# A SwiGLU down projection with seven products for eight in seven of its eleven chunk pairs, summed inside the PSUM banks

## The chip, the cores and the metric

One core of one Trainium2 chip runs the whole kernel in one launch. The metric is the device time of one execution in microseconds; the kernel before takes 1071.21 us (median of three runs, 1068.43 to 1071.74). The engines are TensorE (PE, with its weight loads as PEld), VectorE (DVE), ScalarE (ACT), GpSimd (POOL) and SyncE (SP), which here only issues DMAs.

## What is computed

A decoder trunk of two layers on 512 tokens of width 1024, in float32. Layer 0 mixes with two kinds of attention, layer 1 with pooling; each layer then has a SwiGLU block. The change is in the last product of that block, which runs twice:

```python
def swiglu(h, w_gate, w_up, w_down):
    return (jax.nn.silu(h @ w_gate) * (h @ w_up)) @ w_down   # 512x1024 -> 512x2816 -> 512x1024
...
    h = h + rmsnorm(swiglu(u, ffn_w_gate[layer], ffn_w_up[layer], ffn_w_down[layer]), g[3])
```

The down product multiplies the 512 x 2816 activations by a 2816 x 1024 weight. The 2816 are 22 chunks of 128, taken in 11 pairs.

## The kernel before, in words

**Three matmuls for one product.** PE multiplies in a reduced format, so every float32 operand is split in two: a high half (ACT copies it, rounding) and a low half (the source minus the high half, a subtraction on DVE or POOL). `conv` (L242 to L245) does it for weights, `split` (L219 to L221) for activations. A product is then high x high, high x low and low x high: three matmuls.

**Gate and up.** `Ffn.run` (L933) goes through the 11 pairs of hidden chunks, gate and up in turn, with seven products for eight (Strassen, in Winograd's form): DVE forms sums of weight blocks (`comb`, L913) and of results (L962 to L964, L972), `up_done` (L981 to L987) writes the activations `act`, two tiles of 128 x 512 for a pair: hidden on the partitions, tokens along the row.

**Down.** `down` (L776) has eight PSUM banks, one for each of four token tiles and two halves of the output (tags `psT`, `psO` for half 0, `psA`, `psS` for half 1). It runs through all 22 chunks for half 0, then the first 14 chunks for half 1, and keeps the last eight chunks' weights of half 1 in `wrh`, `wrl`; the returned `tail(t)` finishes one token tile after the other, so that the norm behind can begin. For each chunk, token tile and half there are three matmuls of 128 x 512 (L782 to L784): 22 x 8 x 3 = 528. Activations are split by `split` on ACT and DVE; the low halves of the weights go to POOL and DVE by the pattern `ggv` (two on POOL, one on DVE).

**What sets the order.** The kernel is written with tile pools; a scheduler orders the instructions of each engine when the program is built, and each engine then runs its own list in that order. A buffer of a pool comes free with its last reader. The pools that matter: `wr` (11 raw weight tiles, filled by SP's DMAs), `wq` (14 split weights), `g` (31 tiles), `xe` (4), `jk` (2) and, in attention, `sc` (2).

## Time and profile before

| | us |
|---|---|
| median of three runs | 1071.21 |
| the profiled execution | 1071.16 |
| its span, first to last instruction | 1069.4 |
| PE busy / DVE / ACT / POOL | 1023.3 / 755.3 / 563.0 / 314.5 |
| the two down products, start of the first matmul | 553.08 and 942.64 |

The page's slices show PE at 97% to 100% nearly everywhere, a mean granted clock of 0.987 of full speed, and DVE at 90% or more in the gate and up stages. A matmul's record is longer than its share of the engine, since matmuls overlap: the distance from one start to the next is what one costs in a full stream. The same holds for DVE and ACT records. A view of waits names the instruction that was late, and for whom.

### The profile page before, as it was taken

How to read it: one execution, taken by the hardware profiler on the slowest of the kernel's cores; microseconds unless marked ns; L12 is line 12 of the kernel's file. 1: busy time of each engine (PE TensorE's matmuls, PEld its weight loads, DVE VectorE, ACT ScalarE, POOL GpSimd, SP SyncE). 2: the span in 40 equal slices, each digit the busy share in tenths (PEclk: the TensorE clock that was granted, in tenths of full speed). 3: DMA queues.
4: the chain of work that ended last, by engine and by line, in shares of the span. 5: the costliest groups of instructions: out<-in, count | busy, mean ns of one | idle time of the engine just before them, and what ended most of it. 6: DMA issues, size and time to landing. Idle time of an engine off the chain costs nothing.

```text
span 1069.4 us, 19004 instructions
## 1 busy us (share of the span) xinstructions
PE 1023.3 (96%) x6892; PEld 940.4 (88%) x6892; DVE 755.3 (71%) x1527; ACT 563.0 (53%) x1194; POOL 314.5 (29%) x282
## 2 busy tenths in 40 slices
PE   6999999997999999999999999988999999999997
PEld 5788978896888999999988888988999999978886
DVE  5338898758749999899973153998898898881204
ACT  6437688769656454454564352764444354472401
POOL 5713666767751000000026371420000000053510
PEclk9999999999999999999999999998999999999999
DMA  8841201323531434433343374003342333433302
GB/s 244 195 96 40 60 21 32 95 73 102 169 89 31 119 109 116 123 102 107 119 153 114 106 218 110 21 11 92 97 138 83 112 114 90 139 117 121 108 1 78
DMA packets 156493, 108.58 MB, mean 102 GB/s; under 512 B 14836, under 2 KB 137584, under 8 KB 156400
## 3 DMA queue, kind: packets, MB, share of 16 engines
q1 hardware_dynamic: 155600, 106.23, 34.6%
q8 instruction: 54, 0.88, 0.4%
q10 hardware_dynamic: 800, 1.15, 0.3%
q14 instruction: 39, 0.32, 0.1%
HBM read 101.88 MB, written 2.10 MB: 97 GB/s over the span
## 4 chain that ended last, share of the span: by engine, by line
PE 77%; DVE 8%; ACT 5%; issue 3%; DMA 3%; POOL 2%; SPq 1%; DVEq 0%; POOLq 0%; ACTq 0%
PE psS L944 8%; PE psS L945 8%; PE psS L946 7%; PE psA L944 5%; PE psA L945 5%; PE psA L946 5%; PE psT L784 2%; PE psO L784 2%; PE psT L782 2%; PE psT L783 2%; PE psO L783 2%; PE psO L782 2%; PE psA L782 2%; PE psA L784 2%; PE psA L783 2%
## 5 line engine op out<-in xcount | busy, mean ns | idle before, releaser
L244 ACT ACTIVATE wh<-wr 128x512 fp32r<-128x512 f32 x376 | 226.3, 626 | 256.8 <-DVE wr L913 82.4
L245 POOL TENSOR_TENSOR wl<-wr,wh 128x512 fp32r<-128x512 f32 x101 | 145.4, 1449 | 556.5 <-ACT wh L244 329.8
L245 DVE TENSOR_TENSOR wl<-wr,wh 128x512 fp32r<-128x512 f32 x275 | 189.5, 706 | 92.1 <-ACT wh L244 89.4
L944 PE MATMUL psS<-th,wh 128*128 128x256 f32 x528 | 149.8, 285 | 1.3 <-DVE comb L964 1.3
L945 PE MATMUL psS<-tl,wh 128*128 128x256 f32 x528 | 150.0, 285 | 0.0
L946 PE MATMUL psS<-th,wl 128*128 128x256 f32 x528 | 149.9, 284 | 0.0
L944 PEld LDWEIGHTS psS<-th,wh 128*128 128x128 f32 x528 | 101.6, 193 | 1.6 <-DVE comb L964 0.9
L945 PEld LDWEIGHTS psS<-tl,wh 128*128 128x128 f32 x528 | 101.8, 193 | 0.0
L946 PEld LDWEIGHTS psS<-th,wl 128*128 128x128 f32 x528 | 101.7, 193 | 0.0
L913 DVE TENSOR_TENSOR wr<-wr,wr 128x512 f32<-128x512 f32 x132 | 86.7, 682 | 1.3 <-DMA wr<-in_ffn_w_up_dram 0.5
L946 PE MATMUL psA<-uh,wl 128*128 128x256 f32 x272 | 77.5, 286 | 3.1 <-DVE wl L245 3.0
L944 PE MATMUL psA<-uh,wh 128*128 128x256 f32 x272 | 77.5, 286 | 2.1 <-DVE comb L962 1.7
L945 PE MATMUL psA<-ul,wh 128*128 128x256 f32 x272 | 77.3, 284 | 0.0
L270 POOL TENSOR_SCALAR E<-E,ri 128x128 f32<-128x128 f32 (+3 forms) x48 | 56.0, 1167 | 38.8 <-DVE ri L590 12.9
L584 ACT ACTIVATE E<-E,mn 128x128 f32<-128x128 f32 (+1 forms) x96 | 53.4, 557 | 15.7 <-DVE mn L582 15.0
L946 PEld LDWEIGHTS psA<-uh,wl 128*128 128x128 f32 x272 | 52.6, 194 | 3.5 <-DVE wl L245 3.5
L944 PEld LDWEIGHTS psA<-uh,wh 128*128 128x128 f32 x272 | 52.5, 193 | 2.7 <-DVE comb L962 2.1
L332 PE MATMUL psA<-uh,wh 128*128 128x512 f32 (+1 forms) x136 | 51.4, 378 | 1.7 <-DVE nq L464 1.5
L945 PEld LDWEIGHTS psA<-ul,wh 128*128 128x128 f32 x272 | 52.6, 193 | 0.0
L221 DVE TENSOR_TENSOR pl<-psT,ph 128x512 fp32r<-128x512 f32 (+1 forms) x72 | 42.3, 593 | 12.5 <-ACT ph L220 8.7
L334 PE MATMUL psA<-uh,wl 128*128 128x512 f32 (+1 forms) x136 | 50.9, 374 | 0.0
L333 PE MATMUL psA<-ul,wh 128*128 128x512 f32 (+1 forms) x136 | 50.7, 373 | 0.0
(354 smaller groups left out, 3009.8 us busy)
## 6 DMA issues: line engine op xcount, KB each, us to landing
wr<-in_ffn_w_gate_dram SPq DMA_DIRECT2D x98, 256.0 KB
wr<-in_ffn_w_up_dram SPq DMA_DIRECT2D x98, 256.0 KB
wr<-in_ffn_w_down_dram SPq DMA_DIRECT2D x88, 256.0 KB
wr<-in_attn_w_in_dram SPq DMA_DIRECT2D x40, 256.0 KB
wr<-in_attn_w_out_dram SPq DMA_DIRECT2D x16, 256.0 KB
x<-in_x_dram SPq DMA_DIRECT2D x4, 512.0 KB
gbc<-in_norm_g_dram SPq DMA_DIRECT2D x8, 256.0 KB
h<-in_x_dram SPq DMA_DIRECT2D x4, 512.0 KB
```

Source lines behind the costliest of these rows:

```text
L244: nc.scalar.activation(hi, src, AF.Copy)
L245: next_engine(key).tensor_tensor(lo, src, r32(hi), op=ALU.subtract)
L270: (nc.vector if k == "v" else nc.gpsimd).tensor_scalar(e, e, s1, None, op0=ALU.mult)
L332: nc.tensor.matmul(psum, wh, ah, start=first, stop=False)
L584: nc.scalar.activation(e, e, AF.Exp, bias=mn[:, n_:n_ + 1], scale=-1.0, accum_out=sm[:, n_:n_ + 1])
L782: nc.tensor.matmul(o, acts[c][0][:, tok], wh[k], start=first, stop=False)
L783: nc.tensor.matmul(o, acts[c][0][:, tok], wl[k], start=False, stop=False)
L784: nc.tensor.matmul(o, acts[c][1][:, tok], wh[k], start=False, stop=last)
L913: next_engine("sadd").tensor_tensor(o, x0, x1, op=op)
L944: nc.tensor.matmul(o, wh, bh, start=start and k == 0, stop=False, skip_group_check=True)
L945: nc.tensor.matmul(o, wh, bl, start=False, stop=False, skip_group_check=True)
L946: nc.tensor.matmul(o, wl, bh, start=False, stop=k == 3, skip_group_check=True)
```

## The change

Seven of the eleven pairs (`nst=7`) of the down product are done with seven products for eight. For a pair, with e and o its even and odd activation tile (tokens 0 to 255 and 256 to 511) and b11, b12 (even chunk), b21, b22 (odd chunk) the blocks of the weight, a product is 256 tokens by 512 outputs: two token tiles, six matmuls of 128 x 512.

- `act_sums` forms three sums of activation blocks for each of the seven pairs, on DVE, as soon as the pair's activations are there (128 x 256 each), so in the gate and up stage.
- `down` is a method of its own. A first pass over the seven pairs does four products of each into four pairs of banks (C11 in `psO`, C22 in `psT`, C21 in `psA`, C12 in `psS`), added up over the seven pairs. Then the sums between the products are made once, in the banks: for each of two bank numbers two copies on ACT and four additions on DVE. A second pass does the other three products of each pair. The four remaining pairs are plain: half 0 first, half 1 from kept weights in `tail(t)`, as before.
- For each pair DVE makes three weight sums (L1049, `sub`) in the first pass, and one weight sum and one activation sum in the second; six operands are split in the first pass and five in the second, all low halves on DVE (pattern `v`); none of down's go to POOL any more.
- The block b22 is loaded in both passes: five loads of 256 KB for such a pair in place of four.
- Pools: `g` has 33 tiles, `jk` 3, and `sc` is now taken from `jk`. The bank tags of the pooling mixer change with the banks that come free.

```diff
--- before.py
+++ after.py
@@ -32,13 +32,14 @@
     norm='vggvgvvg',
     wlo0='g',
     wlo1='ggv',
-    ng=31,
+    ng=33,
     no=8,
     xe=4,
     pt=4,
     w=14,
     wr=11,
-    jk=2,
+    jk=3,
+    nst=7,
     psb=(2, 2, 2, 2),
     early=('kc', 'vc'),
     hpe=50,
@@ -60,7 +61,7 @@
     plo='vvv',
     lead=0,
     tr2='W0 T0 T1 E0 T2 E1 B0 T3 E2 E3 W1 B1 M0 M1 F0 F1 B2 M2 B3 R0 M3 A0 F2 F3 R1 Z A1',
-    ptags=(('psO', 'psA'), ('psO', 'psS')),
+    ptags=(('psO', 'psS'), ('psO', 'psA')),
 )
 OFF = {}
 _o = 0
@@ -148,7 +149,7 @@
         return T(shape, "pt", CFG["pt"], dt, label)
 
     def SC():
-        return T([P, S], "sc", 2, F32, "sc")
+        return JK("sc")
 
     def SM(shape, label="sm"):
         return T(shape, "sm", 16, F32, label)
@@ -840,6 +841,7 @@
             self.uns = []
             self.acts = {}
             self.ws = {}
+            self.S = {}
             self.g = bcast(norm_g[layer, 2], "g2", where)
 
         def weights(self, p):
@@ -992,6 +994,8 @@
                     gate_done(ms[i])
                 else:
                     up_done(todo[i][0], ms[i - 1], ms[i])
+                    if pairs.index(todo[i][0]) < CFG["nst"]:
+                        self.act_sums(todo[i][0])
 
             gens = [self.pair_weights(w_, p) for p, w_ in todo]
             ws = [next(gens[0])]
@@ -1009,25 +1013,115 @@
                 middle(ms[i])
             finish_(len(todo) - 1)
 
-            wres = T_([P, 8, S], "uh", 1, F32R, "wrh"), T_([P, 8, S], "ul", 1, F32R, "wrl")
-            pos = []
-
-            def take(shape):
-                pos.append(0)
-                k = len(pos) - 1
-                return tuple(w_[:, k:k + 1, :] for w_ in wres)
-
-            def get(c):
-                if c >= 20:
-                    t_ = XE([P, 2, S], F32R, label="asp")
-                    hi, lo = t_[:, 0, :], t_[:, 1, :]
+            return self.down(pairs)
+
+        def act_sums(self, p):
+
+            e, o = self.acts[2 * p], self.acts[2 * p + 1]
+            a11, a21, a22 = e[:, 0:256], e[:, 256:], o[:, 256:]
+            t_ = G([P, S], label="as")
+            s1, s3 = t_[:, 0:256], t_[:, 256:]
+            nc.vector.tensor_add(s1, a21, a22)
+            nc.vector.tensor_sub(s3, a11, a21)
+            nc.vector.tensor_sub(a21, s1, a11)
+            self.S[p] = t_
+
+        def down(self, pairs):
+
+
+
+
+            w = w_down[self.layer]
+            n = CFG["nst"]
+            C11, C22, C21, C12 = ([BANK(tag) for _ in range(2)] for tag in ("psO", "psT", "psA", "psS"))
+            out_ = {(t, m): ((C11, C12) if t < 2 else (C21, C22))[m][t % 2] for t in range(NT) for m in range(2)}
+
+            def raw(p, k, m):
+                c = 2 * p + k
+                return load_raw(w[c * P:(c + 1) * P, m * S:(m + 1) * S].rearrange("(k p) f -> p k f", p=P), [P, 1, S])[0][:, 0, :]
+
+            def put(src, pair=None):
+                hi, lo = pair or WQ2([P, S])
+                conv(hi, lo, src, "slo")
+                return hi, lo
+
+            def sub(o, x0, x1):
+                nc.vector.tensor_tensor(o, x0, x1, op=ALU.subtract)
+
+            def prod(o, a, b, first=False, last=False):
+                (ah, al), (bh, bl) = a, b
+                nc.tensor.matmul(o, ah, bh, start=first, stop=False, skip_group_check=True)
+                nc.tensor.matmul(o, ah, bl, start=False, stop=False, skip_group_check=True)
+                nc.tensor.matmul(o, al, bh, start=False, stop=last, skip_group_check=True)
+
+            def tile_of(a, j):
+                return tuple(x_[:, j * P:(j + 1) * P] for x_ in a)
+
+            t2s = {}
+            for i, p in enumerate(pairs[:n]):
+                b11, b12, b22 = raw(p, 0, 0), raw(p, 0, 1), raw(p, 1, 1)
+                t1, t2s[p] = JK("t1"), G([P, S], label="t2")
+                e_, s_ = (XE([P, 2, S], F32R, label=l_) for l_ in ("ae", "as"))
+                conv(e_[:, 0, :], e_[:, 1, :], self.acts[2 * p], "slo")
+                w11 = put(b11)
+                sub(t1, b12, b11)
+                sub(t2s[p], b22, t1)
+                w2 = put(t2s[p])
+                sub(b12, b22, b12)
+                conv(s_[:, 0, :], s_[:, 1, :], self.S[p], "slo")
+                w3 = put(b12)
+                w1 = put(t1)
+                ends = i == 0, i == n - 1
+                for o, a, c0, b in ((C11, e_, 0, w11), (C22, e_, 256, w2), (C21, s_, 256, w3), (C12, s_, 0, w1)):
+                    for j in range(2):
+                        prod(o[j], (a[:, 0, c0 + j * P:c0 + (j + 1) * P], a[:, 1, c0 + j * P:c0 + (j + 1) * P]), b, *ends)
+            for j in range(2):
+                x_, y_ = JK("u2"), JK("u3")
+                nc.scalar.activation(x_, C11[j], AF.Copy)
+                nc.vector.tensor_add(x_, C22[j], x_)
+                nc.vector.tensor_add(y_, C21[j], x_)
+                nc.scalar.activation(C21[j], y_, AF.Copy)
+                nc.vector.tensor_add(C22[j], C12[j], y_)
+                nc.vector.tensor_add(C12[j], C12[j], x_)
+            for i, p in enumerate(pairs[:n]):
+                b21, b22 = raw(p, 1, 0), raw(p, 1, 1)
+                e, o = self.acts[2 * p], self.acts[2 * p + 1]
+                o_ = XE([P, 2, S], F32R, label="ao")
+                s_ = G([P, 2, 256], F32R, label="s4")
+                conv(o_[:, 0, :], o_[:, 1, :], o, "slo")
+                w21 = put(b21)
+                sub(t2s[p], b21, t2s[p])
+                w4 = put(t2s[p])
+                sub(e[:, 256:], o[:, 0:256], e[:, 256:])
+                conv(s_[:, 0, :], s_[:, 1, :], e[:, 256:], "slo")
+                w22 = put(b22)
+                for c_, a, b in ((C11, (o_[:, 0, 0:256], o_[:, 1, 0:256]), w21), (C21, (o_[:, 0, 256:], o_[:, 1, 256:]), w4),
+                                 (C12, (s_[:, 0, :], s_[:, 1, :]), w22)):
+                    for j in range(2):
+                        prod(c_[j], tile_of(a, j), b)
+            chunks = [2 * p + k for p in pairs[n:] for k in range(2)]
+            nr = len(chunks)
+            acts = []
+            for i, c in enumerate(chunks):
+                if i < 6:
+                    pair = tuple((C if i < 2 else G)([P, S], F32R, label=l_) for l_ in ("ah", "al"))
                 else:
-                    f = G if c < 10 or c >= 16 else O if c < 14 else C
-                    hi, lo = (f([P, S], F32R, label=n_) for n_ in ("ah", "al"))
-                split(hi, lo, self.acts[c])
-                return hi, lo
-
-            return down(get, NF, w_down[self.layer], lambda i: take)
+                    x_ = XE([P, 2, S], F32R, label="asp")
+                    pair = x_[:, 0, :], x_[:, 1, :]
+                conv(pair[0], pair[1], self.acts[c], "slo")
+                acts.append(pair)
+                b = put(raw(c // 2, c % 2, 0))
+                for t in range(NT):
+                    prod(out_[t, 0], tile_of(pair, t), b, False, i == nr - 1)
+            wres = [T([P, 8, S], tag, 1, F32R, "wres") for tag in ("uh", "ul")]
+            held = [put(raw(c // 2, c % 2, 1), tuple(x_[:, i, :] for x_ in wres)) for i, c in enumerate(chunks)]
+
+            def tail(t):
+                for i in range(nr):
+                    prod(out_[t, 1], tile_of(acts[i], t), held[i], False, i == nr - 1)
+                return [out_[t, 0], out_[t, 1]]
+
+            return tail
 
     T_ = T
     phase["wlo"] = CFG["wlo1"]
```

The scheduler's lists of DVE and PE change as follows, here in the first of the two blocks (the second reads alike). In these rows `wh`/`wl` are the high and low half of a weight, `ae`, `as`, `ao`, `s4` split activations of the passes, `al` the low half of a plain chunk's activation, `t1`, `t2` weight sums, `u2`, `u3` the sums in the banks, `comb` gate and up's results. Lines of the kernel after: L246 low half, L974 the last addition of gate and up, L988 and L989 the last activations, L1049 `sub`, L1081 to L1085 the sums in the banks, L1053 to L1055 high x high, high x low, low x high.

DVE where gate and up end and down begins, before:

```order
L972 TENSOR_TENSOR comb_22_7093<-psS_109_7092,comb_22_7093 128x512
L986 TENSOR_TENSOR act_21_7210<-comb_21_6988,comb_22_7093 128x256
L987 TENSOR_TENSOR act_22_7211<-comb_21_6988,comb_22_7093 128x512
L221 TENSOR_TENSOR al_1_7234<-act_1_4123,ah_1_7233 128x512
L221 TENSOR_TENSOR asp_1_7673<-act_21_7210,asp_1_7673 128x512
```

The same place in the kernel after:

```order
L974 TENSOR_TENSOR comb_22_7121<-psS_109_7120,comb_22_7121 128x512
L988 TENSOR_TENSOR act_21_7238<-comb_21_7016,comb_22_7121 128x256
L989 TENSOR_TENSOR act_22_7239<-comb_21_7016,comb_22_7121 128x512
L1049 TENSOR_TENSOR t2_1_7258<-wr_167_7255,t1_1_7257 128x512
L1049 TENSOR_TENSOR t2_2_7315<-wr_170_7312,t1_2_7314 128x512
L1049 TENSOR_TENSOR t2_3_7372<-wr_173_7369,t1_3_7371 128x512
L246 TENSOR_TENSOR ae_2_7316<-act_1_4123,ae_2_7316 128x512
L246 TENSOR_TENSOR as_9_7317<-as_2_5004,as_9_7317 128x512
L246 TENSOR_TENSOR wl_200_7270<-t2_1_7258,wh_200_7269 128x512
```

Where `al_1`, which the first chunk needs, stood right behind the last activations, three weight sums and two low halves now stand ahead of `wl_200`, which the second product of the first pair needs.

DVE between the two passes, in the kernel after; the list is continuous, and these are its 89th to 100th instruction from the L974 above:

```order
L246 TENSOR_TENSOR s4_7_7923<-act_13_6244,s4_7_7923 128x256
L246 TENSOR_TENSOR al_3_8005<-act_17_6794,ah_3_8004 128x512
L246 TENSOR_TENSOR al_4_8027<-act_18_6795,ah_4_8026 128x512
L1082 TENSOR_TENSOR u3_1_7651<-psA_52_7247,u2_1_7650 128x512
L1049 TENSOR_TENSOR t2_7_7600<-wr_198_7918,t2_7_7600 128x512
L246 TENSOR_TENSOR al_5_8049<-act_19_7067,ah_5_8048 128x512
L1081 TENSOR_TENSOR u2_2_7658<-psT_97_7246,u2_2_7658 128x512
L246 TENSOR_TENSOR al_6_8071<-act_20_7068,ah_6_8070 128x512
L246 TENSOR_TENSOR wl_234_7764<-t2_3_7372,wh_234_7763 128x512
L246 TENSOR_TENSOR wl_235_7771<-wr_191_7752,wh_235_7770 128x512
L246 TENSOR_TENSOR al_2_7983<-act_16_6522,ah_2_7982 128x512
L246 TENSOR_TENSOR wl_236_7801<-wr_192_7792,wh_236_7800 128x512
```

Five low halves of plain chunks (`al`), which no matmul needs before the second pass is over, stand ahead of `wl_236`, which the second pass's fourth pair needs.

PE at the place that needs it, in the kernel after; the fourth row is the 198th of the 486 matmuls of down:

```order
L1053 MATMUL psA_52_7247<-wh_234_7763,ao_3_7754 128x512
L1054 MATMUL psA_52_7247<-wl_234_7764,ao_3_7754 128x512
L1055 MATMUL psA_52_7247<-wh_234_7763,ao_3_7754 128x512
L1054 MATMUL psO_37_7243<-wl_236_7801,ao_4_7796 128x512
L1055 MATMUL psO_37_7243<-wh_236_7800,ao_4_7796 128x512
L1054 MATMUL psO_38_7244<-wl_236_7801,ao_4_7796 128x512
L1053 MATMUL psS_110_7249<-wh_229_7686,s4_1_7671 128x512
```

From this row on 289 matmuls of down follow, itself included.

## Rows read from the trace of the kernel before

**Rows 1.** The page's busy times (us, share of the span, instructions).

```profile
PE 1023.3 (96%) x6892; PEld 940.4 (88%) x6892; DVE 755.3 (71%) x1527; ACT 563.0 (53%) x1194; POOL 314.5 (29%) x282
```

**Rows 2.** Busy time by stretch: PE, PEld, DVE, ACT, POOL, granted clock, DMA share, GB/s.

```profile
500.00:530.00 30.00, 30.00 (x252) 30.00 (x251) 28.17 (x52) 15.16 (x28) 0.00 (x0) 1.00 0.39 114
560.00:590.00 30.00, 30.00 (x134) 24.82 (x134) 11.52 (x22) 14.22 (x27) 19.49 (x8) 1.00 0.36 114
960.00:990.00 30.00, 30.00 (x134) 24.82 (x134) 5.23 (x7) 6.99 (x12) 10.78 (x8) 1.00 0.40 124
```

**Rows 3.** PE's waits from 330 to 1064 us: total, times, longest.

```profile
PE psA L946 <- DVE wl L245: 3.0, 1, 3.0
PE psT L782 <- ACT ah L220: 2.3, 2, 1.2
...
PE psT L784 <- DVE al L221: 0.4, 2, 0.2
```

**Rows 4.** Timeline of PE, the second down: start, length, idle before.

```profile
941.19 0.28 PE L946 MATMUL psS<-uh,wl 128*128 128x256 f32 x1
942.64 0.50 PE L782 MATMUL psT<-wh,ah 128*128 128x512 f32 x1 [1.17 <-ACT ah L220]
...
944.96 0.50 PE L784 MATMUL psT<-wh,al 128*128 128x512 f32 x1 [0.21 <-DVE al L221]
...
1062.05 0.39 PE L784 MATMUL psS<-wrh,asp 128*128 128x512 f32 x1
...
1062.73 0.39 PE L784 MATMUL psS<-wrh,asp 128*128 128x512 f32 x1
```

**Rows 5.** Timeline of DVE, instructions in close succession.

```profile
500.31 0.41 DVE L964 TENSOR_TENSOR comb<-psS,comb 128x256 f32<-128x256 f32 x1
500.64 0.68 DVE L245 TENSOR_TENSOR wl<-wr,wh 128x512 fp32r<-128x512 f32 x1
...
558.88 7.91 DVE L221 TENSOR_TENSOR al<-act,ah 128x512 fp32r<-128x512 f32 x13
```

**Rows 6.** Timeline of DVE at the end of the first gate and up.

```profile
542.65 0.69 DVE L245 TENSOR_TENSOR wl<-wr,wh 128x512 fp32r<-128x512 f32 x1 [0.99 <-ACT wh L244]
...
545.77 0.69 DVE L245 TENSOR_TENSOR wl<-wr,wh 128x512 fp32r<-128x512 f32 x1 [1.56 <-ACT wh L244]
...
551.94 0.69 DVE L972 TENSOR_TENSOR comb<-psS,comb 128x512 f32<-128x512 f32 x1 [1.50 <-PE psS L946]
552.66 1.47 DVE L986 TENSOR_TENSOR act<-comb,comb 128x256 f32<-128x256 f32 x1
554.06 0.68 DVE L987 TENSOR_TENSOR act<-comb,comb 128x512 f32<-128x512 f32 x1
```

**Rows 7.** DVE's groups by shape, 350 to 545 us: busy us, mean ns, idle.

```profile
L245 DVE TENSOR_TENSOR wl<-wr,wh 128x512 fp32r<-128x512 f32 x112 | 74.3, 683 | 3.6 <-ACT wh L244 3.5
...
L972 DVE TENSOR_TENSOR comb<-psS,comb 128x512 f32<-128x512 f32 x20 | 13.7, 686 | 3.3 <-PE psS L946 3.2
...
L963 DVE TENSOR_TENSOR comb<-psS,comb 128x256 f32<-128x256 f32 x21 | 8.7, 418 | 1.3 <-PE psS L946 1.2
```

**Rows 8.** Timeline of ACT, high halves in close succession.

```profile
557.31 2.23 ACT L220 ACTIVATE ah<-act 128x512 fp32r<-128x512 f32 x4
```

**Rows 9.** Stretches in attention: PE busy, granted clock, DMA share, GB/s.

```profile
248.00:250.00 2.00, 0.08 (x1) 1.00 0.58 133
250.00:252.00 2.00, 2.00 (x7) 0.58 0.06 9
252.00:254.00 2.00, 2.00 (x10) 0.57 0.63 215
```

**Rows 10.** The chain of waits, 230 to 240 us: start, length, what.

```profile
233.92 2.59 DMA wr<-in_attn_w_out_dram
```

**Rows 11.** Six stretches of attention, 90 to 270 us, the last and the sum.

```profile
240.00:270.00 30.00, 24.26 (x147) 21.45 (x145) 24.80 (x71) 27.01 (x69) 20.74 (x21) 0.90 0.33 96
sum 180.00, PE 170.60 PEld 152.24 DVE 145.97 ACT 141.13 POOL 117.28; mean PE 28.43 PEld 25.37 DVE 24.33 ACT 23.52 POOL 19.55
```

## The prediction

> **What bounds the kernel now.** I read the page's busy times first: PE is at 96% of the span, DVE at 71%, ACT at 53% [rows 1]. A mean over stages says little, so next came busy time by stretch. In gate and up PE is full and DVE nearly so, 28.17 of 30 us; in down PE is full too, but DVE has 5 to 12 us of work in 30 and POOL 11 to 19 [rows 2]. So down is bound by PE alone, with DVE free, while gate and up have PE ahead of a DVE with little room. The view of waits agrees: from 330 us on PE waits only for single events, 3.0 us once in gate and up, and in down 2.3 + 0.4 us for both blocks together, or 1.4 us each [rows 3]. The timeline of PE then gives the price of a matmul of 128 x 512: three steps in 1062.73 - 1062.05 = 0.68 us, so 0.227 us each [rows 4]. Down of the second block reaches from the end of gate and up (941.19 + 0.28 = 941.47) to the last start plus a step (1062.96): 121.5 us [rows 4], of which 528 x 0.2267 = 119.7 us are matmuls.
>
> The sum is made against the profiled execution, 1071.16 us, with a span of 1069.4 us and 1.8 us around it; the median of the runs, 1071.21 us, is the same number for this purpose.
>
> **What the change takes away.** A pair has 2 chunks x 8 tiles x 3 = 48 matmuls; with seven products it has 7 x 2 x 3 = 42. Seven pairs save 42 matmuls, 9.5 us a block, 19.0 us in all, at PE's step. Were nothing late, that would be the gain, since PE sets the pace of down.
>
> **What it adds, and DVE's price.** One DVE record of 128 x 512 lasts 683 ns, one of 128 x 256 418 ns [rows 7], but that is not its cost in a stream: thirteen of them take 7.91 us [rows 5], so (7.91 - 0.68) / 12 = 0.60 us from start to start; a narrow one costs 500.64 - 500.31 = 0.33 us [rows 5]. The Trainium skill says otherwise ("VectorE: DVE Perf Modes", section "The DRAIN you can't avoid"): the next operation does not start before the pipe of the one in front is empty. The rows disagree, 0.60 against 0.68, and the measurement decides; by the page's rule every DVE row would cost its whole record, which is the upper end further down.
>
> By pair, the first pass has six low halves and three sums, 9 x 0.60 = 5.4 us of DVE, against 24 matmuls, 5.4 us of PE. The second has four wide low halves and a narrow one, a wide and a narrow sum, 5 x 0.60 + 2 x 0.33 = 3.7 us, against 18 matmuls, 4.1 us. So DVE, which had between a sixth and two fifths of its time taken in down [rows 2], is now exactly as loaded as PE, before the sums in the banks and the plain chunks' halves. Where two engines are equally loaded, the order decides, and there I count along DVE's list.
>
> **Entry.** T0 is the end of gate and up on PE. DVE starts their last addition at T0 + 0.04 (551.90 to 551.94) and the next, which reads its result, 0.72 us later [rows 6]. A narrow activation, a wide one, three weight sums and two low halves follow (0.33 + 6 x 0.60), then `wl_200`, ready at T0 + 5.4 (0.04 + 0.72 + 0.33 + 3.6 + 0.68). PE has six matmuls with high halves to fill in, 1.4 us, after the first weight sum (T0 + 2.4) and its high half on ACT (0.6). So it is idle for 4.0 us where it was idle for 1.4. (551.94 to 554.06 was slower in the trace: the narrow one took 1.47 us, once, while POOL was at work [rows 6]; down's POOL work goes.)
>
> **First pass.** The last low half of the pass is the 72nd of DVE's list from T0: 0.76 for the addition, 11 narrow ones (3.6), 60 wide ones (36.2): T0 + 40.6. PE has only 162 matmuls there (six of the 168 were done before T0), 36.7 us. Its idle time is 4.6 us by then, most of it from the entry: the load is equal and the lead never comes back.
>
> **Between the passes.** DVE's list goes on with halves of the second pass, the sums in the banks and, ahead of what PE needs next, five low halves of plain chunks. `wl_236` is the 100th: 28 more, 22 wide (13.3), 3 narrow (1.0) and three additions from PSUM, taken at 0.69 for their record [rows 7] (2.0): T0 + 57.0 with its record. PE can have done 191 matmuls after T0, 43.3 us: idle time is now 13.7 us. Behind `wl_236`, 289 matmuls are left, 65.5 us. DVE needs 20 more instructions for the rest of the second pass, 12 us, and PE comes to the last of these after 92 matmuls, 21 us: from there DVE leads, and the plain chunks and `tail` run at PE's pace.
>
> **Sum.** T0 to the end of down: 57.0 + 65.5 = 122.5 us. The six early matmuls push T0 itself by 1.4 us. Against 121.5 that is +2.4 us a block: 42 matmuls less, and 11.9 us more waiting. Waits on ACT and on semaphores inside these sums I take at 0.5 us a block (ACT takes 2.23 / 4 = 0.56 us for a high half [rows 8], less than DVE's 0.60 for the low one). Two blocks: +5.8.
>
> **Smaller terms.** Three narrow sums in gate and up are 1.0 us of DVE for a pair, whose PE time is two runs of 84 matmuls at 30 / 252 = 0.12 us [rows 2], 20.2 us; the free 1.83 in 30 us [rows 2] is 1.2 in 20.2, so it just fits. Taken at 0; if not, seven pairs cost up to 7 us a block, and below nothing it can't be, since it only adds. The rows that prepare down before T0 (ten, 5.8 us) meet DVE's idle time there, at least 0.99 + 1.56 + 1.50 us [rows 6]; cost 0, counted in the entry if not. Loads: 51 for 44; DMA stands at 0.36 to 0.40 of its share [rows 2], so the bytes are covered; one load takes 2.59 us [rows 10], and some second-pass blocks are asked for five DVE rows (3 us) ahead. Taken at 0, bounded by some 0.5 us for each of seven pairs. The new sharing of `sc` with `jk` shuffles attention's order: PE is idle there for 180 - 170.6 = 9.4 us [rows 11], which is the most it could gain and, with nothing nearer, the most I let it lose; taken at 0.
>
> Clock: after 2 us in which PE was busy for 0.08, the granted clock was 0.58 and 0.57 for the next 4 us, the 1.2 GHz level for most of it [rows 9], 1.7 us lost. The entry's idle time, 3.0 us in one piece, may do the same. But the loss lies ahead of waits that DVE's list sets at T0 + 40.6 and + 57.0, and these swallow it: 0. The Trainium skill has the rule ("TensorE: Matmul & The Clock Gate", section "Part 1: The HAM clock gate (the "warmup" mystery)"): an idle array falls back to half its clock. The trace agrees, 0.57; by the rule alone the two entries would add 3.4 us.
>
> **Bounds.** Were DVE never late, PE would wait as now at the entry and for one chain of sums between the passes, two copies of 0.56 and two additions of 0.69 [rows 7, 8], 2.5 us: -9.5 + 2.5 = -7.0 a block, 1057.2 us. If each DVE row cost its record (14 x 0.42 + 86 x 0.68 = 64.4): 64.4 + 65.5 + 1.4 - 121.5 = +9.8 a block, 1090.8 us. I take 0.60, the nearest row. **Forecast 1071.2 + 5.8 = 1077.0 us.** A difference of 0.3%, 3.2 us, is about what a measurement of this kernel can tell from none.
>
> **Rivals.**
> 1. *DVE keeps ahead, and the matmuls are won*: 1057.2 us. For it: the small slack that I am 2.4 us short of; DVE's idle time ahead of T0 [rows 6]. Against it: the list has no gap to catch up in, and 9 x 0.60 against 24 x 0.227 leaves none. It decides from where `wl_236` comes before T0 + 54.6, and is whole at T0 + 46. Chance 0.13 for any gain over 3.2 us.
> 2. *The two terms cancel*: `wl_236` at 54.6, 4% earlier than I count, or attention gains 5 us. Within 3.2 us: 1071. Chance 0.23.
> 3. *DVE's rows cost their record*, by holds between dependent rows (0.72 instead of 0.60 [rows 6]), late blocks or the sums in gate and up: between 1083 and 1090.8, say 1086 us. For it: nearly every row now reads what ACT or the row in front has just made. Against: gate and up have the same mix and run at 0.60. Chance 0.2.
> 4. My forecast, 1074.5 to 1083: chance 0.44.
>
> Faster 0.13; within 0.3% 0.23; slower 0.64. The range, 1063 to 1088 us, leaves out the far halves of rivals 1 and 3; the forecast's own is 1074 to 1082.
>
> **What would show it.** In the profile after: 486 matmuls of 0.227 us in each down; DVE near 100% in the first 60 us of down and POOL at none; PE waiting for some 4 us at the entry, for DVE's low halves, and for 8 to 10 us in pieces of 0.5 to 3 between the passes, some 14 us a block; no wait from about T0 + 57 on. T0 to the end of down near 122.5 us. It would be wrong if PE waits under 10 us a block, if gate and up grow by more than 2 us, or if attention moves by more than 3 us.

## The result, and the profile after

The changed kernel takes 1102.67 us (median of four runs, 1098.90 to 1104.49), beside it the kernel before 1070.83; the ratio is 1.0296, with a 95% interval of 1.0261 to 1.0332. It is 32 us slower; 6 were forecast. The profiled execution has a span of 1099.3 us against 1069.4.

First the busy times on the page, the answer to [rows 1] (us, share of the span, instructions):

```profile
PE 1027.1 (93%) x6808; PEld 935.7 (85%) x6808; DVE 872.1 (79%) x1784; ACT 599.1 (55%) x1272; POOL 224.4 (20%) x223
```

84 matmuls fewer, as meant, and yet PE is not busy for less time; 117 us of work have come to DVE and 90 have left POOL. Next the busy time by stretch, in the columns of [rows 2]: a piece of gate and up, then the whole first down in two pieces, cut where DVE's hundredth row after T0 ends.

```profile
500.00:530.00 30.00, 29.76 (x248) 29.56 (x247) 27.94 (x52) 13.61 (x26) 0.00 (x0) 1.00 0.38 107
565.50:622.40 56.90, 48.17 (x193) 37.34 (x192) 56.71 (x101) 37.42 (x69) 0.00 (x0) 0.94 0.38 117
622.40:688.50 66.10, 66.09 (x291) 54.41 (x292) 44.48 (x75) 37.31 (x72) 15.01 (x13) 1.00 0.63 187
```

The reader is to see how close the count of down came: DVE has 101 rows in 56.9 us without a gap, the hundredth done at T0 + 56.8 (forecast 57.0). A count of a stretch takes in the rows that reach over its edges; by their starts, 191 matmuls lie between T0 and that moment (forecast 191) and 289 behind it (forecast 289 in 65.5 us), in 66.0 us. PE's waits in the first down (total, times, longest):

```profile
PE psT L1053 <- ACT wh L245: 3.7, 1, 3.7
PE psO L1054 <- DVE wl L246: 3.4, 2, 2.3
PE psA L1053 <- ACT psA L1083: 0.7, 1, 0.7
PE psA L1054 <- DVE wl L246: 0.5, 1, 0.5
PE psO L1053 <- ACT wh L245: 0.5, 1, 0.5
```

The loss was elsewhere. The starts of PE's first and last matmul of each stage, read from its timeline, divide the span (us; "attention" is all ahead of the output projection, "mixer" the way from the last matmul of the first down to the first of the second gate and up):

| stage | before | after | difference |
|---|---|---|---|
| attention | 270.1 | 277.0 | +6.9 |
| output projection and norm | 68.0 | 68.8 | +0.8 |
| gate and up, layer 0 | 213.4 | 219.5 | +6.0 |
| down, layer 0 | 121.5 | 122.8 | +1.3 |
| mixer | 40.5 | 45.4 | +4.9 |
| gate and up, layer 1 | 227.6 | 236.3 | +8.8 |
| down, layer 1 | 121.5 | 122.8 | +1.3 |

Down lost 1.3 us each time, or 2.7 with the six early matmuls that now lie in gate and up (1.4 us). The other 24.6 of the 29.9 us are in stages whose own matmuls the change leaves as they are. PE's waits after 330 us, the answer to [rows 3], show the new places:

```profile
PE psT L312 <- DVE tl L222: 7.7, 4, 4.2
PE psT L1053 <- ACT wh L245: 7.4, 2, 3.7
PE psO L1054 <- DVE wl L246: 5.7, 4, 2.3
PE psA L946 <- ACT comb L956: 3.5, 11, 0.7
...
PE psS L1220 <- DVE vl L1197: 1.4, 1, 1.4
...
PE psT L312 <- ACT un L301: 1.0, 1, 1.0
```

In the kernel before, the first of them was this row, which [rows 3] leaves out:

```profile
PE psT L311 <- DVE tl L221: 5.3, 5, 1.7
```

So PE now waits up to 4.2 us at once for `tl`, early in the second gate and up, where 1.7 was the longest. The waits of L946 for ACT's `comb` (gate and up, eleven times) and of L312 for `un` (mixer) weren't there before, and those for `vl` (L1220, mixer) were 0.6 us in all.

### The profile page after: what moved, and what is told of

It reads as the page before. It is cut to its first block, busy times and chain, and to the rows that moved or that the text cites. A ratio compares the mean times of both kernels' runs of the same rounds, so it can differ in the third digit from the quotient of the medians.

```text
span 1099.3 us, 19204 instructions
## 1 busy us (share of the span) xinstructions
PE 1027.1 (93%) x6808; PEld 935.7 (85%) x6808; DVE 872.1 (79%) x1784; ACT 599.1 (55%) x1272; POOL 224.4 (20%) x223
## 4 chain that ended last, share of the span: by engine, by line
PE 74%; DVE 10%; ACT 6%; DMA 3%; issue 3%; POOL 1%; SPq 1%; DVEq 0%; POOLq 0%; ACTq 0%
PE psS L948 8%; PE psS L947 7%; PE psS L946 7%; PE psA L946 5%; PE psA L948 4%; PE psA L947 4%; PE psS L1053 2%; DVE wl L246 2%; PE psO L1054 2%; PE psO L1053 2%; PE psS L1054 2%; PE psS L1055 2%; PE psO L1055 2%; PE psA L1053 2%; PE psO L636 2%
## 5 line engine op out<-in xcount | busy, mean ns | idle before, releaser
L246 DVE TENSOR_TENSOR wl<-wr,wh 128x512 fp32r<-128x512 f32 x322 | 218.4, 696 | 11.8 <-ACT wh L245 11.7
L946 PE MATMUL psS<-th,wh 128*128 128x256 f32 x528 | 151.2, 287 | 0.0
L246 POOL TENSOR_TENSOR wl<-wr,wh 128x512 fp32r<-128x512 f32 x54 | 72.1, 1345 | 362.8 <-ACT wh L245 361.2
L282 POOL TENSOR_TENSOR rs<-ms,mhalf 128x1 f32<-128x1 f32 x32 | 19.2, 601 | 420.5 <-DVE ms L278 387.9
L946 PEld LDWEIGHTS psS<-th,wh 128*128 128x128 f32 x528 | 102.8, 195 | 0.8 <-DVE comb L966 0.4
L946 PE MATMUL psA<-uh,wh 128*128 128x256 f32 x272 | 76.5, 285 | 0.0
L946 PE MATMUL psA<-th,wh 128*128 128x256 f32 x176 | 50.6, 289 | 3.5 <-ACT comb L956 3.5
L946 PEld LDWEIGHTS psA<-uh,wh 128*128 128x128 f32 x272 | 51.9, 192 | 0.2
```

Source lines behind the costliest of these rows:

```text
L246: next_engine(key).tensor_tensor(lo, src, r32(hi), op=ALU.subtract)
L946: nc.tensor.matmul(o, wh, bh, start=start and k == 0, stop=False, skip_group_check=True)
```

## The experiments

Each kernel was timed beside the kernel before on one chip. The table has the ratio with its interval, and the stages of each profile as above (attention, output projection, gate and up, down, mixer, gate and up, down).

| kernel | us | ratio (95%) | att | out | g/u 0 | down 0 | mix | g/u 1 | down 1 |
|---|---|---|---|---|---|---|---|---|---|
| e1_pools | 1089.9 | 1.0163 (1.0133 to 1.0194) | 278.3 | 68.8 | 214.5 | 121.5 | 45.3 | 232.8 | 121.5 |
| e2_own_sc | 1091.4 | 1.0184 (1.0160 to 1.0208) | 267.3 | 68.4 | 217.1 | 127.7 | 40.3 | 231.4 | 128.0 |
| e3_no_sums | 1097.5 | 1.0248 (1.0226 to 1.0270) | 277.3 | 68.8 | 216.9 | 122.8 | 45.2 | 234.9 | 122.8 |
| e4_old_tags | 1101.6 | 1.0277 (1.0250 to 1.0303) | 278.1 | 70.0 | 220.0 | 124.1 | 45.2 | 235.7 | 122.9 |
| e5_jk3 | 1074.6 | 1.0058 (1.0040 to 1.0076) | 270.7 | 68.8 | 214.6 | 121.6 | 42.9 | 228.7 | 121.6 |
| e6_pool_low | 1126.0 | 1.0541 (1.0510 to 1.0571) | 278.2 | 70.1 | 219.3 | 133.7 | 46.4 | 234.3 | 135.2 |
| e7_split | 1095.8 | 1.0266 (1.0228 to 1.0304) | 269.2 | 74.0 | 218.6 | 124.4 | 49.4 | 226.4 | 124.6 |
| e9_split_low_sums | 1120.3 | 1.0480 (1.0445 to 1.0516) | 269.3 | 73.5 | 218.6 | 133.7 | 53.6 | 228.1 | 136.6 |
| e10_less_dve | 1084.5 | 1.0148 (1.0106 to 1.0190) | 275.8 | 68.8 | 219.4 | 115.9 | 45.5 | 234.1 | 115.4 |
| e12_sc_jk3 | 1086.5 | 1.0151 (1.0122 to 1.0179) | 279.1 | 69.7 | 216.0 | 121.6 | 42.9 | 227.5 | 121.6 |
| e13_t1_sc | 1090.4 | 1.0192 (1.0158 to 1.0226) | 268.1 | 67.7 | 217.1 | 127.6 | 40.3 | 231.4 | 127.7 |
| e14_t2_buffer | 1078.2 | 1.0067 (1.0043 to 1.0091) | 269.9 | 67.8 | 215.9 | 123.3 | 40.3 | 230.9 | 122.6 |
| e15_late_plain | 1110.7 | 1.0373 (1.0346 to 1.0399) | 270.0 | 68.8 | 216.2 | 121.7 | 77.8 | 230.9 | 121.3 |

Stages that two kernels run in the same order differ by 1 to 3 us between these single profiles (attention with `sc` as its own pool: 267.3 to 270.7); a smaller difference of a stage is read only where PE's waits show what makes it.

**Theory and rival.** The theory is that each stage outside down lost its time by itself: to the pool settings, to the sums in gate and up, to the bank tags. The rival is that down's load, or chance, did it.

### The pools alone, and the change without them

```diff
 e1_pools: the kernel before, with
-        return T([P, S], "sc", 2, F32, "sc")
+        return JK("sc")
-    ng=31, jk=2,
+    ng=33, jk=3,
 e2_own_sc: the changed kernel, with these lines turned back
```

> The kernel before with only the pools of the change: `sc` takes its buffers from `jk` (3 instead of 2 and 2), `ng` 33; no Strassen in down, old bank tags. PE's list up to gate and up is then that of the changed kernel, word for word. Theory A (the time lost outside down is each stage's own: attention lost 6.9 us, 270.13 to 276.98, by the new order alone): start of the output projection at 277, kernel 1078 us. Rival B (attention's 6.9 us are chance or come from something else in the change): start at 270, 1071 us.

> The changed kernel with the pools of the kernel before (`sc` its own 2 buffers, `jk` 2, `ng` 31); PE's list up to gate and up is that of the kernel before. Theory A: output projection starts at 270 instead of 277, kernel 1096 us, 6.9 below the changed one; the rest as in the changed kernel. Rival B: 1102 to 1103 us.

The pools alone make the kernel before 19 us slower, well over the 7 expected: attention +8.1, mixer +4.8, second gate and up +5.3, the downs nothing. PE's waits in attention of e1_pools are those of the changed kernel:

```profile
PE psS L577 <- DVE mn L582: 4.9, 3, 3.1
PE psT L606 <- DVE pl L221: 3.8, 7, 1.1
PE psS L577 <- DMA fkA<-fkA: 3.6, 2, 3.3
PE psO L635 <- ACT ph L220: 1.4, 3, 0.7
PE psO L635 <- DVE pl L221: 0.8, 1, 0.8
```

In the changed kernel the first of them reads 4.9, 3, 3.1 as well; before it was:

```profile
PE psS L577 <- DVE mn L582: 2.0, 3, 0.9
```

With the old pools (e2) attention and the mixer are as they were, but down is 5 us a block longer: down wanted the buffers. So the settings of the pools are about 20 of the 30 us, and turning all of them back gains 11 us, no more.

### Which pool

```diff
 e5_jk3: the kernel before, with
-    jk=2,
+    jk=3,
 e12_sc_jk3: the same, and
-        return T([P, S], "sc", 2, F32, "sc")
+        return JK("sc")
```

> The kernel before with `jk` 3 instead of 2 and nothing else (`sc` has its own two buffers, `ng` 31). Theory A (the third buffer of `jk` lets VectorE run the products `mq` of the next row group ahead of the `vl` that PE waits for in the mixer stage, while attention loses by the sharing of `sc`): output projection at 270 as before, last matmul of down to first of gate and up 45 instead of 40.5 us, kernel about 1076 to 1080 us. Rival B (the sharing of `sc`, or `ng`, does the harm in both places): 40.5 us there, kernel 1071 us.

> The kernel before with `sc` out of `jk` and `jk` 3, `ng` left at 31: e1_pools without the two more buffers of `g`. Theory A (sharing costs what e1_pools lost beyond e5_jk3, some 15 us): 1087 to 1091 us, attention 277 to 278 us to the start of the output projection. Rival B (`ng` 33 reorders attention): attention 270 us, kernel 1075 us.

A third `jk` costs 0.58% (mixer +2.4, and 1 to 2 us in places), the sharing of `sc` on top of it another 0.9%, 8.4 us of it in attention. That difference is far outside the scatter: with `sc` as its own pool attention takes 267.3 to 270.7 us in eight profiles, with `sc` out of `jk` 275.8 to 279.1 in seven. (The sharing also leaves three buffers for what had five in e5; which of the two it is wasn't separated.) Of `ng` only the profiles speak: 2.4 us in the mixer and 5.3 in the second gate and up between e12 and e1, while the intervals of these two overlap (and with `ng` 33 eight transposes, under 1 us, lie in gate and up instead of the mixer).

PE's waits in e5_jk3 from the mixer into the second gate and up show the third buffer's price:

```profile
PE psT L311 <- DVE tl L221: 6.0, 2, 4.8
PE psA L944 <- DVE act L868: 1.5, 1, 1.5
```

In the kernel before, the first of these is 2.9 us there (two waits, 1.7 the longest) and the second isn't there; a wait of 3.0 us for `wl`, [rows 3], is there and not in e5. Two groups of DVE in the mixer stage of e5_jk3, its weight sums for the next gate and up (busy us, mean ns, idle before), and below them the same two of the kernel before, hint at what the buffer does:

```profile
L913 DVE TENSOR_TENSOR wr<-wr,wr 128x512 f32<-128x512 f32 x5 | 3.3, 679 | 0.0
L913 DVE TENSOR_TENSOR s<-wr,wr 128x512 f32<-128x512 f32 x3 | 2.0, 679 | 0.0
```

```profile
L913 DVE TENSOR_TENSOR s<-wr,wr 128x512 f32<-128x512 f32 x2 | 2.4, 1200 | 0.0
L913 DVE TENSOR_TENSOR wr<-wr,wr 128x512 f32<-128x512 f32 x3 | 2.0, 677 | 0.0
```

Eight sums, where the kernel before has five: work for later, let in by a free buffer while PE is about to wait for DVE. That is a reading; it was not tried by itself.

### The bank tags, and the sums in gate and up

```diff
 e4_old_tags: the changed kernel, with
-    ptags=(('psO', 'psS'), ('psO', 'psA')),
+    ptags=(('psO', 'psA'), ('psO', 'psS')),
 e3_no_sums: the changed kernel, with
-            nc.vector.tensor_add(s1, a21, a22)
-            nc.vector.tensor_sub(s3, a11, a21)
-            nc.vector.tensor_sub(a21, s1, a11)
-            self.S[p] = t_
+            self.S[p] = self.acts[2 * p + 1]
```

> The changed kernel with the bank tags of the kernel before in the pooling mixer (psO, psA and psO, psS). Theory A (the new tags reorder the mixer stage, and the two waits of 0.98 and 1.42 us with 7 us of half clock behind them come from that): last matmul of down to first of gate and up 41 instead of 45.4 us, kernel 1098 us. Rival B (the banks of the new down come free in another order, and the old tags would wait for the last of them): 47 us or more there, kernel 1104 us or more.

> The changed kernel without the three sums of activations in gate and up (act_sums computes nothing; down takes the activations themselves, so the output is another). Theory A (these 21 DVE rows a block delay DVE, PE waits for it and loses its clock): gate and up shrink from 219.5 and 236.3 to about 215 and 229 us, kernel 1091 us. Rival B (DVE's rows that prepare down, or the clock at the start of the block, are the cause; the sums fit into DVE's idle time): gate and up within 1.5 us of 219.5 and 236.3, kernel 1101 us.

The tags do nothing: the mixer takes 45.4 and 45.2 us, so neither side was right there, and e1 and e5 show where its time went. Without the sums gate and up are 2.6 and 1.4 us shorter, and the eleven short waits of L946 for `comb`, 3.5 us, are gone. The 1.4 alone would be within the scatter (234.1 to 236.3 us among kernels with the sums and these pools); the waits are what carries it. The theory had 12 us for the sums, the rival 3 at most; they are 4.

### Does DVE's list set the time of down?

```diff
 e6_pool_low: the changed kernel, with
-                conv(hi, lo, src, "slo")     # in put(), down's weights: DVE
+                conv(hi, lo, src, "wlo")     # 'ggv': two of three on GpSimd
 e10_less_dve: the changed kernel, with
-                sub(t1, b12, b11)
-                sub(t2s[p], b22, t1)
+                sub(t2s[p], b22, b11)
...
-                sub(b12, b22, b12)
...
-                w3 = put(b12)
-                w1 = put(t1)
+                w3 = w1 = put(b12)
```

> The changed kernel with two of three low halves of down's weights on GpSimd (the pattern that the kernel before has there), all else as it is. Theory A (VectorE's list sets the pace of down to the end of the second pass, 122.9 us a block): down falls to 114 to 118 us a block, kernel 1090 us. Rival B (waits on single events at the entry and between the passes are there whoever computes the low halves, and GpSimd's row of 1.3 to 1.7 us is later than VectorE's of 0.68): down 122 us or more, kernel 1102 us or more.

> The changed kernel with 21 VectorE rows of 128x512 fewer in the first pass of each down: of the three weight sums one is left (t2 = b22 - b11), and the third and fourth product share the halves of b12, so the output is another. PE's matmuls, their order and the loads stay. Theory A (the count along VectorE's list sets when PE gets on; 21 x 0.60 = 12.6 us off it takes the row that the second pass waits for from T0 + 57 to T0 + 44, where PE is not yet): down 113 to 116 us a block instead of 122.9, kernel 1085 to 1090 us. Rival B (PE's waits are the entry and the chain of sums between the passes, which stay): down 120 to 122 us, kernel 1097 to 1101 us.

e6 came out against the theory: down grew by 11 to 12 us, which the rival's "122 us or more" covers, but for the greater part by a cause that neither side had. The timelines of DVE and then of GpSimd in its first pass show it (start, length):

```profile
583.53 1.77 DVE L246 TENSOR_TENSOR ae<-act,ae 128x512 fp32r<-128x512 f32 x1
585.22 1.78 DVE L1049 TENSOR_TENSOR t<-wr,wr 128x512 f32<-128x512 f32 x1
586.92 1.50 DVE L1049 TENSOR_TENSOR act<-act,act 128x256 f32<-128x256 f32 x1
588.35 1.75 DVE L246 TENSOR_TENSOR wl<-wr,wh 128x512 fp32r<-128x512 f32 x1
590.02 0.68 DVE L1049 TENSOR_TENSOR t<-wr,t 128x512 f32<-128x512 f32 x1
```

```profile
581.32 3.43 POOL L246 TENSOR_TENSOR wl<-t,wh 128x512 fp32r<-128x512 f32 x2
584.72 3.43 POOL L246 TENSOR_TENSOR wl<-wr,wh 128x512 fp32r<-128x512 f32 x2
588.11 1.44 POOL L246 TENSOR_TENSOR wl<-t,wh 128x512 fp32r<-128x512 f32 x1
```

In this stretch a wide DVE row lasts 1.75 to 1.78 us instead of 0.68 and the narrow one (586.92) 1.50 instead of 0.42, one for each of GpSimd's, and the row at 590.02, after GpSimd's end, has its 0.68 again. The Trainium skill has this as a rule ("SBUF — State Buffer", section "SBUF: two separate sides"): a VectorE operation with two inputs in SBUF and a GpSimd one hold the port pair that they share one after the other, each for its whole length. The trace agrees, 1.77 against 0.68 us. It shows the other side as well: in another stretch DVE's rows keep their 0.68, and a row of GpSimd, 1.28 us long in other places, becomes the long one, for which PE then has its longest wait in this down:

```profile
604.17 8.26 POOL L246 TENSOR_TENSOR wl<-wr,wh 128x512 fp32r<-128x512 f32 x1 [4.26 <-ACT wh L245]
```

```profile
PE psO L1054 <- POOL wl L246: 5.2, 1, 5.2
```

This second part the rival had named (GpSimd's half comes later). From T0 to the first of the sums written into the banks (L1084) the engines of e6 were busy as follows (columns of [rows 2]):

```profile
567.91:632.15 64.24, 48.00 (x175) 36.30 (x176) 56.81 (x72) 35.87 (x68) 45.03 (x23) 0.90 0.28 95
```

DVE has 72 rows there, where the changed kernel has 100 in 56.7 us, and is busy for as long with them; the other 7.4 us it is idle, for a late load and a half of GpSimd's. The work that left DVE's list gave it no time.

e10 takes rows away and moves none, and down fell to 115.9 and 115.4, where the theory had 113 to 116 and the rival 120 to 122. (With the 21 rows go seven high halves on ACT, which was busy for 37 of 57 us in the changed kernel, and the buffers of the sums; these weren't taken apart.) Its waits in the first down:

```profile
PE psT L1053 <- ACT wh L245: 3.7, 1, 3.7
PE psA L1053 <- ACT psA L1080: 0.5, 1, 0.5
```

The waits for `wl` between the passes are gone, the entry's is the same. For the second down, 480 matmuls x 0.2267 + 3.5 idle + 3.4 of clock = 115.7, near its 115.4 (a stretch's loss of clock is the sum, over its microseconds, of what the granted clock lacks to 1); 12.6 us of DVE's rows went and some 7 us of each down with them, since these terms are left. So the loss of clock, which was without effect as long as DVE came later, counts as soon as DVE doesn't.

### Pools sorted by stage, and GpSimd once more

```diff
 e7_split: the changed kernel, with
-        return JK("sc")
+        return T([P, S], "sc", 2, F32, "sc")
-        junk = [JK("mq") for _ in range(2)]
+        junk = [SC() for _ in range(2)]
-    ng=33,
+    ng=31,
 e9_split_low_sums: e7_split, the edit of e6_pool_low, and the sums of act_sums as
+            nc.gpsimd.tensor_tensor(s1, a21, a22, op=ALU.add)
...
 e13_t1_sc: e2_own_sc, with
-                t1, t2s[p] = JK("t1"), G([P, S], label="t2")
+                t1, t2s[p] = SC(), G([P, S], label="t2")
```

> The changed kernel with `sc` as its own two buffers, which the products `mq` of the post-norms use too, `jk` 3 for the sums of down and the weight sums, `ng` 31: the same memory. Theory A (attention and the mixer stage lose by the pools, down wants the third `jk`): output projection at 267 to 270, mixer stage 40.3 us, down 122.9 us; kernel 1081 to 1085 us. Rival B (down wants `ng` 33, not `jk`): attention and mixer as in A, down 127 to 128 us, kernel 1091 us.

> The pools of e7_split, the low halves of e6_pool_low, and the three sums of activations in gate and up on GpSimd, which is idle there. If the terms add as theory A has them (pools -19, low halves -6 a block, sums -5): 1065 to 1070 us, at or just under the kernel before. If GpSimd's rows come late or hold up VectorE's: 1080 us or more.

> e2_own_sc (the changed kernel with the old pools) with one more edit: the weight sum t1 takes its buffer from `sc`, which is idle in down, instead of `jk`. Theory A (in e2_own_sc two buffers for t1, u2 and u3 together made down 4.9 us a block longer than in the changed kernel): down 123 to 124.5 instead of 127.9 us, rest as there, kernel 1083 to 1085 us. Rival B (`ng` 31 instead of 33 or the chain of sums u2, u3 made it longer): down 127 to 128 us, kernel 1091 us.

e7 gave attention and most of down what the theory said (269.2; 124.4 and 124.6), but with `mq` in buffers of their own the stretch behind the output projection became 5.9 and the mixer 8.9 us longer than before. So no arrangement is free in the stages that it was not made for. e9 shows the sums on GpSimd to be worth nothing (gate and up 218.6 as in e7), and down as long as in e6. e13 went to the rival: t1's buffer doesn't matter; what down got from `jk` 3 in e7 is then left to u2, u3 and the weight sums, which wasn't separated.

### The entry, and the plain chunks

```diff
 e14_t2_buffer: e2_own_sc, with
-                t1, t2s[p] = JK("t1"), G([P, S], label="t2")
+                t1, t2s[p] = JK("t1"), (G([P, S], label="t2") if i else T([P, S], "t2a", 1, F32, "t2"))
-                x_, y_ = JK("u2"), JK("u3")
+                x_, y_ = SC(), JK("u3")
 e15_late_plain: e14_t2_buffer, with
-                if i < 6:
-                    pair = tuple((C if i < 2 else G)([P, S], F32R, label=l_) for l_ in ("ah", "al"))
+                if i >= 4:
+                    pair = tuple((C if i < 6 else G)([P, S], F32R, label=l_) for l_ in ("ah", "al"))
```

> e2_own_sc with two edits: the weight sum t2 of the first pair of each down has a buffer of its own (in the changed kernel it waits for one of `g`, which gate and up hold to their end), and u2 comes from `sc` instead of `jk`. Theory A (the entry's wait of 3.7 us and the half clock behind it come from that one buffer; two more for u2 and u3 shorten the chain between the passes): no wait over 1 us at the entry, down 116 to 119 us instead of 127.9, no matmul of down ahead of T0, kernel 1066 to 1072 us. Rival B (what VectorE does not do at the entry it has to do later, since its list is as long): entry shorter, waits between the passes longer, down 122 to 125 us, kernel 1080 us.

> e14_t2_buffer with the halves of the first four plain chunks in the buffers that the second pass uses (so that VectorE can't take them up ahead of it) and those of the last four where the first were. Theory A (the plain chunks' low halves ahead of the second pass's weights are what PE waits for between the passes): 2 to 3 us a block less than e14_t2_buffer, 1062 to 1068 us. Rival B (the chain of sums is what ends last there, or the plain chunks come late in turn): within 1.5 us a block of e14_t2_buffer, or longer.

The timeline of DVE at the entry of the changed kernel, the answer to [rows 6], shows what e14 starts from:

```profile
561.74 0.41 DVE L966 TENSOR_TENSOR comb<-psS,comb 128x256 f32<-128x256 f32 x1
565.59 0.69 DVE L974 TENSOR_TENSOR comb<-psS,comb 128x512 f32<-128x512 f32 x1 [3.43 <-PE psS L948]
566.38 0.43 DVE L988 TENSOR_TENSOR act<-comb,comb 128x256 f32<-128x256 f32 x1
566.72 0.68 DVE L989 TENSOR_TENSOR act<-comb,comb 128x512 f32<-128x512 f32 x1
567.33 1.29 DVE L1049 TENSOR_TENSOR t<-wr,t 128x512 f32<-128x512 f32 x2
```

DVE is idle for 3.4 us right ahead of T0 and takes up the sum t2, on which PE waits, only after it. With a buffer of its own t2 comes ahead of T0, and in e14 PE has no wait at the entry. Its waits in that down are:

```profile
PE psO L1054 <- DVE wl L246: 3.5, 2, 2.0
PE psT L1053 <- ACT wh L245: 2.2, 1, 2.2
PE psT L1054 <- DVE wl L246: 1.9, 1, 1.9
PE psO L1053 <- ACT wh L245: 0.5, 1, 0.5
```

The first of them comes 31 us after T0, and their sum is 8.1 us; in the changed kernel it is 8.7. From T0 to the end e14 has all 486 matmuls ahead of it and takes 123.3 and 122.6, the changed kernel with six done already 122.8, or 124.2 with them: 0.9 and 1.6 us saved of some 5.4 (3.7 of wait, 1.7 of clock). That is the rival: what DVE does earlier at the entry PE waits for later. But e14 also has `jk` 2 and `ng` 31. Against e2, from which it is one step away, its downs are 5.8 and 6.8 us shorter (the six early matmuls counted in e2), by two edits at once; no run has the buffer of t2 alone, so what the entry by itself is worth isn't shown. All in all e14 is 24 us below the changed kernel, about half of it by the old pools (e2) and half by its two buffers; it is the best version with seven products found, and still 0.4% to 0.9% slower than the kernel before.

e15 takes another 1.6 and 1.3 us off each down, less than the theory's 2 to 3, about the rival's 1.5, and no more than what one profile differs from another, so the order of the plain chunks stays undecided. The plain chunks, though, now hold to the end of down the `xe` buffers into which the mixer's band matrices are loaded (PE's waits in the mixer, and then those of SyncE's DMA queue ahead of it):

```profile
PE psO L1220 <- ACT vh L1195: 19.5, 2, 18.8
```

```profile
SPq L1171 <- PE psT L1055: 22.8, 4, 21.8
```

The load of the bands waits 21.8 us for the last readers of a plain chunk, ACT and DVE wait in their order behind the load, and PE for them: one wait of 18.8 us, and 22.2 us of clock lost in that stage, for a buffer that was chosen for the stage ahead.

## Why the prediction was wrong in size

**Right: what sets down.** T0 to the end of down was put at 122.5 us and is 122.8; the row that ends DVE's lead was put at T0 + 57.0, and the matmul behind it starts at 622.39, T0 + 56.8 (T0 = 565.27 + 0.28). e10 shows the cause: 12.6 us of DVE rows fewer, and 7 us of down go. The price of a row, 0.60 us, held (56.71 us for 101 rows, narrow ones among them). By then PE had 191 matmuls done, 43.3 us of the 56.8: 13.5 us lost for 13.7 forecast, of which 8.7 are waits and 3.4 the clock. (The 4.6 us that the prediction puts down as idle by the end of the first pass don't follow from its own 40.6 and 36.7, which leave 3.9; no term of the sum uses them.) "PE waits under 10 us a block" was named as a sign against the step; it came true and was a bad sign, since the clock's part isn't told as waiting. The other two signs, gate and up longer by more than 2 us and attention moved by more than 3, came true as well (6.0 and 8.8, and 6.9 us), and they were good ones.

**Right: the entry and the clock.** 3.7 us of waiting at the entry for 4.0 forecast, and the loss of clock behind it was swallowed by DVE's list, as said. e10 shows the condition; what an entry without a wait gives back, 0.9 and 1.6 us in e14 against the changed kernel, was measured only together with other pools.

**Failed: "The new sharing of `sc` with `jk` shuffles attention's order ... taken at 0".** It costs 8.4 us (e5 to e12), and attention as a whole is 6.9 us longer in the changed kernel: near the bound of 9.4 that stood beside it. The middle of a range between a gain and a loss of 9.4 us was taken for want of a nearer row, and the order alone, which could be read, didn't say which side it would be.

**Failed: no term for the mixer and for the other stages that share the pools.** `jk` serves the products `mq` of every norm and the weight sums of gate and up. The prediction followed the pools only where `sc` had moved. The third `jk` and the two more `g` cost 4.8 us in the mixer, and all three settings together 5.3 in the second gate and up and 0.8 behind the output projection (e1, e5, e12). The reading that PE waits "only for single events" from 330 us on passed over the largest of them, five waits for `tl` of 5.3 us in all; the longest grew from 1.7 to 4.8 us by the third `jk` alone (e5).

**Failed in size: the three sums in gate and up, "it just fits. Taken at 0".** They cost 2.6 and 1.4 us, inside the bound of 7 a block, in short waits of PE for `comb`, at most one a pair (3.5 us in eleven waits).

Put together, from the stage tables: the pools alone +20.0 (e1, span 1089.4 for 1069.4); on top of them the change itself +9.9 (1099.3 - 1089.4), of which 4.0 are the sums. The other 5.9 stand against a forecast of 5.8. So close a match is in part luck: the two downs with their early matmuls are 5.4 of it, and the rest is what is left of differences in gate and up and attention that single profiles can't tell. The forecast priced what the change is about, and took at nothing what it does beside that.

**The rivals.** That DVE keeps ahead is refuted by the profile: `wl_236` is done at T0 + 56.8, not before T0 + 54.6, and PE waits for it; e10 had to take rows away to come near it. That the two terms cancel needed that row earlier or a gain in attention; attention lost. That DVE's rows cost their record is refuted by the 101 rows in 56.9 us; of the third rival only the sums in gate and up were there, at 4.0 us. The Trainium skill ("VectorE: DVE Perf Modes", section "The DRAIN you can't avoid") says behind the sentence that the prediction took from it that a next operation which isn't held starts earlier; the prediction left this out, so 0.60 us for a record of 0.68 doesn't contradict the section.

**Open.** Why the order with a shared `sc` is slower in attention (its longer waits for `mn` and `pl` are seen, the buffer that makes them is not), which use of `jk` and `g` lengthens the mixer, what e7's own buffers for `mq` upset, and what the entry's wait costs by itself.

## What to carry to other kernels

A buffer count or a shared pool is a change of its own, to every stage that draws from the pool: build the kernel before with these settings alone and compare its order and time, ahead of any sum on the algorithm. Where a helper engine is as loaded as the one that it feeds, count its rows up to the point where the lead returns: here 12.6 us of rows taken off it bought 7 us, until the matmuls, the entry and the clock were what is left. And a free engine is only free if using it leaves the busy one's rows as long as they were, and its own rows in time.

## What the runs showed of the hardware

The strength of one thing was not expected: with GpSimd in the same stretch, VectorE's wide rows took up to 1.78 us for 0.68, or one row of GpSimd 8.26 for 1.28 (e6), so that moving two of three low halves away made down 11 to 12 us longer. The kernel before has GpSimd at work in down and shows 1.4 us of waits a block in it; VectorE has time to spare there, 5 to 12 us of work in 30 [rows 2].

Of the clock: in the mixer of the changed kernel PE was busy for 0.87 and 0.73 us of two stretches of 2 us (waits of 0.98 and 1.42 us), and then ran at the 1.2 GHz level for over 5 us, as these rows show (PE, PEld, DVE, ACT, POOL, granted clock, DMA share, GB/s).

```profile
704.00:706.00 2.00, 0.87 (x6) 0.43 (x5) 1.88 (x3) 1.36 (x3) 1.65 (x3) 1.00 0.00 0
706.00:708.00 2.00, 0.73 (x4) 0.73 (x4) 2.00 (x3) 1.49 (x3) 0.66 (x1) 0.72 0.00 0
708.00:713.00 5.00, 5.00 (x25) 5.00 (x25) 1.23 (x3) 0.72 (x1) 0.55 (x1) 0.50 0.01 3
```

Two waits of 2.4 us together so cost 3.4 us of clock on top, where 0.6 us of waiting and no loss of clock were before: 5.2 us, about the mixer's 4.9, and a wait is not only its own length where nothing behind it swallows the clock.
